# A decoder layer in split fp32: the indexer's second token half first, and 256-column fp32 products as two of 128

## The chip, the cores and the metric

The kernel runs on one core of a Trainium2 chip. The metric is the device time of one execution, in microseconds (us); lower is better.

## The reference

One layer of a hybrid decoder over 256 tokens of 2048 channels, all in float32. Cut to what matters here:

```python
h = rmsnorm(x, g_mix)
u_pool, q, k, v, q_idx, k_idx, w_idx = split(h @ w_in)
pool_out = pool_mixer(u_pool, w_pool, pool_scale)      # trailing means of 2/4/8/16 tokens, a map per group
# attention with an indexer: 16 heads of 64 score every causal key, the best 64 keys of a query stay
dots  = einsum('bqhd,bsd->bhqs', q_idx, k_idx)
score = einsum('bqh,bhqs->bqs', w_idx * idx_scale, relu(dots))
_, sel = top_k(where(causal, score, -inf), 64)
logits = einsum('bqhd,bqkhd->bhqk', q, k[sel]) * 128 ** -0.5 + bias      # 8 heads of 128
out    = einsum('bhqk,bqkhd->bqhd', softmax(logits), v[sel])
x = x + concat(pool_out, out) @ w_out
x = x + conv_ffn(rmsnorm(x, g_ffn))                    # 2048 -> 2 x 5632 -> 2048
x = x + (p @ w_ple_proj) * sigmoid(rmsnorm(x, g_ple) @ w_ple_gate)
return rmsnorm(x, g_final)
```

## The kernel before, in words

Activations lie channel-major: 128 channels on the partitions, the 256 tokens on the free axis. Exactness comes from splitting: every fp32 operand is a rounded part `hi` and a rest `lo`, both of type fp32r, and a weight tile of 128 x 128 costs two products. L147 multiplies the `hi` weights with 512 columns (hi and lo of the 256 tokens), L148 the `lo` weights with 256 columns. This pair L147, L148 makes up most of the program; a **step** below is the time from one L147 to the next with one L148 between.

Weights arrive in **units** of up to 1024 columns (512 KB, eight pairs): SyncE (SP) loads one into `raw` (four buffers), ScalarE (ACT) casts it to `hi` (L87), VectorE (DVE) subtracts to get `lo` (L88), and TensorE (PE) consumes both, from one of three `w` buffers in turn. So L147 waits for the cast of its unit and L148 for the subtraction.

The stages are, in order: v and the indexer's keys; the indexer (`query`, `score`), the q and k tiles (`qk_tile`) with the top-k on VectorE, `logits`, `softmax`; then the pool columns with the second half of `softmax`, the transposes and the products with v (`attend`), and `pool_map` (L483, twelve products of 256 columns); w_out; ffn up and down; the gate.

Three functions multiply in other shapes. `score` makes, for each of two heads, products of 128 columns (first half of the tokens) and of 256 columns (second half), in fp32r. `logits` and `attend` use operands of plain fp32; such a product stands in the profile as two instructions. The second half's `logits` (L393) have 256 columns, those of the first half 128; `attend` has one of 256 (L444) and one of 128 (L446) for each head.

The program is written as a list of operations and a scheduler decides, from its own estimate of times, in which order each engine gets them; the engines then run their lists strictly in order and wait for each other by semaphores. So an edit in one product can move others on every engine. Buffers in PSUM: four `pa` for the projections, four `ps` for everything else.

Of the kernel before, what the change touches and what calls it, by code (L numbers as in the profile page):

```python
# [18 lines left out]
P = 128  # L19
S = 256  # L20
# [30 lines left out]
def layer(ctx: ExitStack, tc: tile.TileContext, a: dict):  # L51
    nc = tc.nc
    in_order = tc.keep_in_program_order
    V, A, T, G = nc.vector, nc.scalar, nc.tensor, nc.gpsimd
# [152 lines left out]
    with ExitStack() as c1:  # L207
# [8 lines left out]
        qk = ar.tile([P, 2 * NH, S], F32, name="qk", tag="qkA")  # L216
# [43 lines left out]
        v = ar.tile([P, 2, NH * P], F32, name="v")  # L260
# [5 lines left out]
        for n in range(3):  # L266
            w = NVK if n < 2 else NVK - 80
            for t in range(2):
                vs = v[:, t, n * NVK:n * NVK + w]
# [35 lines left out]
        def score(j, qr):  # L305
            pds = [aux.tile([P, 512], F32, name="ps") for _ in range(2)]
            for e in range(2):
                for t, (o, n) in enumerate(((0, P), (P, S))):
                    q = qr[:, e, t * P:(t + 1) * P]
                    T.matmul(pds[e][:, o:o + n], q, kr[:, :n], start=True, stop=False)  # L310
                    T.matmul(pds[e][:, o:o + n], q, kr[:, S:S + n], start=False, stop=True)  # L311
            for e in range(2):
                h = 2 * j + e
                rl = ar.tile([P, 384], F32, name="rl", bufs=2)
                A.activation(rl, pds[e][:, :384], AF.Relu, scale=1.0 / 32.0)
                for t in range(2):
                    src = s0[t] if h == 0 else sc[t]
                    V.scalar_tensor_tensor(sc[t], rl[:, :P] if t == 0 else rl[:, P:],
                                           wx[:, t, h:h + 1], src, op0=OP.mult, op1=OP.add)
# [5 lines left out]
        for j in range(IH // 2):  # L325
            ps = cm_tile(a["w_qi"], j) if j else ps_q
            if j == 0:
                index_keys()
            qxs.append(query(ps))
            if j >= 2:  # L330
                score(j - 2, qxs[j - 2])
        for j in range(2):
            qk_tile(j)
            score(j + 6, qxs[j + 6])
# [53 lines left out]
        def logits(t, h0):  # L388
            n = P * (t + 1)
            hb = 512 // n  # L390
            pl = aux.tile([P, 512], F32, name="ps")
            for h in range(h0, h0 + hb):
                T.matmul(pl[:, (h - h0) * n:(h - h0 + 1) * n],  # L393
                         qk[:, 2 * h, t * P:(t + 1) * P], qk[:, 2 * h + 1, :n],
                         start=True, stop=True)
            hs = slice(h0, h0 + hb)
            V.scalar_tensor_tensor(L[t][:, hs, :], pl.rearrange("p (h s) -> p h s", s=n), P ** -0.5,
                                   tb[:, hs, S - n:], op0=OP.mult, op1=OP.add)
# [22 lines left out]
        for j in range(12, 16):  # L421
            qk_tile(j)
            if j >= 14:
                h0 = 4 * (j - 14)
# [15 lines left out]
        def attend(h, pt):  # L440
            po = aux.tile([P, 512], F32, name="ps")
            for e in range(2):
                vs = slice((h + e) * P, (h + e + 1) * P)
                T.matmul(po[:, e * S:(e + 1) * S], v[:, 0, vs], pt[:, e, :S],  # L444
                         start=e == 0, stop=False, skip_group_check=True)
                T.matmul(po[:, e * S + P:(e + 1) * S], v[:, 1, vs], pt[:, e, S:],  # L446
                         start=False, stop=e == 1, skip_group_check=True)
            po2 = po.rearrange("p (e s) -> p e s", s=S)
            split(catA[:, h:h + 2, :S], catA[:, h:h + 2, S:], po2)
# [41 lines left out]
        for i, g in enumerate((3, 2, 1, 0)):  # L491
            u = ar.tile([P, 2, PAD + S], F32, name="pu", bufs=2)
            G.memset(u[:, :, :PAD], 0.0)
            for j in range(2):
                cm_evict(u[:, j, PAD:], cm_tile(a["w_u"], 2 * g + j))
                if i < 2:
                    h0 = 4 * i + 2 * j
                    logits(1, h0)
                    softmax(1, slice(h0, h0 + 2))
                else:  # L500
                    h0 = 4 * (i - 2) + 2 * j
# [264 lines left out]
```

## Time and profile before

| | |
|---|---|
| time, median of 3 runs | 1181.37 us (1181.3 to 1181.61) |
| the profiled execution | 1181.5 us, of which the traced span is 1179.7 us |
| PE busy | 1168.7 us, 99% of the span |
| DVE, ACT busy | 855.8 us (73%), 643.8 us (55%) |
| granted TensorE clock | 0.997 in the mean: 2.4 GHz but for the first microseconds and the very end |
| DMA | 194 GB/s in the mean |

TensorE's busy time is a union of instructions that overlap in the record, so that "busy" does not say how fast it goes: what counts is the distance from the start of one product to the start of the next.

### The profile page before, as it was taken

What the parts mean: (1) busy time and instruction counts of PE and PEld (TensorE: products, weight loads), DVE (VectorE), ACT (ScalarE), POOL (GpSimd) and SP (SyncE); (2) the same over time, 40 slices, a digit from 0 to 9 for tenths busy, and PEclk for the clock granted to TensorE, in tenths of its full rate; (3) what the DMA queues carried; (4) which work ended last, traced back from release to release, by engine and by line L of the source; (5) the groups of instructions that cost most, each with busy time, mean ns of one, the idle gap of its engine ahead of it and who ended that gap; (6) DMA issues with size and microseconds to landing.
All of it is one profiled execution on the core that took longest, in us unless ns stands there. A gap on an engine that the chain in (4) does not pass through costs nothing.

```text
span 1179.7 us, 17843 instructions
## 1 busy us (share of the span) xinstructions
PE 1168.7 (99%) x6792; PEld 1035.6 (88%) x6792; DVE 855.8 (73%) x1314; ACT 643.8 (55%) x941; POOL 8.9 (1%) x27
## 2 busy tenths in 40 slices
PE   9999999999999999999999999999999999999996
PEld 9988888898888888888888888888888888888886
DVE  6578977977778888888888888888555555555564
ACT  7466444555546666666665666666444444444563
POOL 0000000000000000000000000000000000000000
PEclk9999999999999999999999999999999999999998
DMA  9656665446565555555555555556666666667662
GB/s 317 211 174 194 242 205 175 163 145 201 193 200 193 190 194 193 195 194 194 194 191 196 193 194 194 192 195 192 195 190 190 194 196 192 193 192 228 190 210 80
DMA packets 67077, 229.09 MB, mean 194 GB/s; under 512 B 7888, under 2 KB 10072, under 8 KB 66864
## 3 DMA queue, kind: packets, MB, share of 16 engines
q1 hardware_dynamic: 63840, 222.04, 58.4%
q10 hardware_dynamic: 2144, 3.28, 0.9%
q0 software_dynamic: 1008, 2.64, 0.6%
q8 instruction: 53, 0.87, 0.3%
q14 instruction: 32, 0.26, 0.1%
HBM read 224.77 MB, written 3.68 MB: 194 GB/s over the span
## 4 chain that ended last, share of the span: by engine, by line
PE 99%; DMA 0%; DVE 0%; ACT 0%; SPq 0%; POOLq 0%; issue 0%; DVEq 0%
PE pa L147 55%; PE pa L148 28%; PE pa L175 3%; PE pa L174 3%; PE pa L176 3%; PE ps L175 1%; PE ps L176 1%; PE ps L174 1%; PE ps L483 0%; PE ps L393 0%; DMA raw<-in_w_first 0%; PE ps L147 0%; PE ps L310 0%; PE ps L311 0%; PE ps L608 0%; PE ps L444 0%
## 5 line engine op out<-in xcount | busy, mean ns | idle before, releaser
L88 DVE TENSOR_TENSOR w<-raw,w 128x1024 fp32r<-128x1024 f32 (+3 forms) x420 | 503.1, 1198 | 216.3 <-ACT w L87 209.8
L147 PE MATMUL pa<-hT,w 128*128 128x512 f32 x1904 | 652.2, 390 | 0.0
L87 ACT CAST w<-raw 128x1024 fp32r<-128x1024 f32 (+3 forms) x420 | 433.3, 1032 | 339.3 <-PE pa L148 249.9
L148 PE MATMUL pa<-hT,w 128*128 128x256 f32 x1904 | 528.7, 278 | 0.0
L147 PEld LDWEIGHTS pa<-hT,w 128*128 128x128 f32 x1904 | 357.3, 188 | 74.7 <-issue 0.6
L148 PEld LDWEIGHTS pa<-hT,w 128*128 128x128 f32 x1904 | 357.9, 188 | 0.3
L147 PE MATMUL pa<-aT,w 128*128 128x512 f32 x704 | 239.4, 389 | 0.0
L148 PE MATMUL pa<-aT,w 128*128 128x256 f32 x704 | 194.3, 276 | 0.0
L147 PEld LDWEIGHTS pa<-aT,w 128*128 128x128 f32 x704 | 132.1, 188 | 27.7
L148 PEld LDWEIGHTS pa<-aT,w 128*128 128x128 f32 x704 | 132.1, 188 | 0.0
L163 ACT COPY eb<-pa 128x256 f32<-128x256 f32 x119 | 44.4, 373 | 140.2 <-PE pa L148 140.1
L164 DVE TENSOR_TENSOR eb<-pa,eb 128x256 f32<-128x256 f32 x119 | 50.3, 423 | 60.8 <-ACT eb L163 60.7
L175 PE MATMUL pa<-w,hT 128*128 128x512 f32 (+2 forms) x178 | 65.0, 365 | 0.0
L176 PE MATMUL pa<-w,hT 128*128 128x512 f32 (+2 forms) x178 | 64.6, 363 | 0.0
L174 PE MATMUL pa<-w,hT 128*128 128x512 f32 (+2 forms) x178 | 58.4, 368 | 0.1
L550 ACT ACTIVATE cv<-ub,cnv 128x256 f32<-128x256 f32 x88 | 52.8, 602 | 0.2
L147 PE MATMUL pa<-catP,w 128*128 128x512 f32 x128 | 45.9, 391 | 0.0
L147 PE MATMUL pa<-catA,w 128*128 128x512 f32 x128 | 45.6, 390 | 0.0
L554 DVE SCALAR_TENSOR_TENSOR cv<-ub,cnv,cv 128x256 f32<-128x256 f32 x88 | 42.6, 485 | 3.0
L552 DVE SCALAR_TENSOR_TENSOR cv<-ub,cnv,cv 128x256 f32<-128x256 f32 x88 | 41.9, 478 | 0.0
L165 DVE TENSOR_TENSOR ub<-eb,rbc 128x256 f32<-128x256 f32 x88 | 37.3, 425 | 2.9
L175 PEld LDWEIGHTS pa<-w,hT 128*128 128x128 f32 x178 | 33.8, 190 | 4.5 <-DVE w L88 0.6
(175 smaller groups left out, 844.7 us busy)
## 6 DMA issues: line engine op xcount, KB each, us to landing
raw<-in_w_up SPq DMA_DIRECT2D x176, 512.0 KB, 4.7
raw<-in_w_down SPq DMA_DIRECT2D x80, 512.0 KB, 4.0
raw<-in_w_qk SPq DMA_DIRECT2D x32, 512.0 KB, 4.1
raw<-in_w_out SPq DMA_DIRECT2D x32, 512.0 KB, 4.2
raw<-in_w_pg SPq DMA_DIRECT2D x32, 512.0 KB, 4.4
raw<-in_w_first SPq DMA_DIRECT2D x15, 552.0 KB, 5.1
raw<-in_w_qi SPq DMA_DIRECT2D x16, 512.0 KB, 3.8
raw<-in_w_u SPq DMA_DIRECT2D x16, 512.0 KB, 3.8
```

Of the source, the lines that this page charges most:

```text
L87: A.copy(hi, raw[:, :n])
L88: V.tensor_sub(lo, raw[:, :n], hi.bitcast(F32))
L147: T.matmul(ps, hi[:, w], act, start=first and i == 0, stop=False)
L148: T.matmul(ps[:, :S], lo[:, w], act[:, :S], start=False, stop=last and i == len(acts) - 1)
L163: A.copy(b, ps[:, S:])
L164: V.tensor_add(b, ps[:, :S], b)
L174: T.matmul(pss[t][:, :n], xh, hi[:, w], start=first and i == 0, stop=False)
L175: T.matmul(pss[t][:, :n], xh, lo[:, w], start=False, stop=False)
L176: T.matmul(pss[t][:, :n], xl, hi[:, w], start=False, stop=last and i == len(kts) - 1)
L550: A.activation(t, u[:, 2:], AF.Identity, bias=cnv[:, k + 3:k + 4], scale=cnv[:, k + 2:k + 3])
L552: V.scalar_tensor_tensor(t, u[:, 1:S + 1], cnv[:, k + 1:k + 2], t, op0=OP.mult, op1=OP.add)
L554: V.scalar_tensor_tensor(t, u[:, :S], cnv[:, k:k + 1], t, op0=OP.mult, op1=OP.add)
```

## The change

In `score` the four products of a head are issued with the second half of the tokens (256 columns) first and the first half (128 columns) last. In `logits` each product of 256 columns becomes two of 128, and in `attend` the product of 256 columns with the first half of v becomes two of 128. Sums, operands and outputs are the same.

```diff
         def score(j, qr):
             pds = [aux.tile([P, 512], F32, name="ps") for _ in range(2)]
             for e in range(2):
-                for t, (o, n) in enumerate(((0, P), (P, S))):
+                for t, o, n in ((1, P, S), (0, 0, P)):
                     q = qr[:, e, t * P:(t + 1) * P]
                     T.matmul(pds[e][:, o:o + n], q, kr[:, :n], start=True, stop=False)
                     T.matmul(pds[e][:, o:o + n], q, kr[:, S:S + n], start=False, stop=True)
...
             for h in range(h0, h0 + hb):
-                T.matmul(pl[:, (h - h0) * n:(h - h0 + 1) * n],
-                         qk[:, 2 * h, t * P:(t + 1) * P], qk[:, 2 * h + 1, :n],
-                         start=True, stop=True)
+                for k0 in range(0, n, P):
+                    c0 = (h - h0) * n + k0
+                    T.matmul(pl[:, c0:c0 + P], qk[:, 2 * h, t * P:(t + 1) * P],
+                             qk[:, 2 * h + 1, k0:k0 + P], start=True, stop=True)
...
                 vs = slice((h + e) * P, (h + e + 1) * P)
-                T.matmul(po[:, e * S:(e + 1) * S], v[:, 0, vs], pt[:, e, :S],
-                         start=e == 0, stop=False, skip_group_check=True)
+                for t in range(2):
+                    ts = slice(t * P, (t + 1) * P)
+                    T.matmul(po[:, e * S + t * P:e * S + (t + 1) * P], v[:, 0, vs], pt[:, e, ts],
+                             start=e + t == 0, stop=False, skip_group_check=True)
                 T.matmul(po[:, e * S + P:(e + 1) * S], v[:, 1, vs], pt[:, e, S:],
                          start=False, stop=e == 1, skip_group_check=True)
```

The lines behind the edits are counted on by up to three in the changed kernel (L393 is then L395, L444 is L447, L446 is L449, L483 is L486).

The scheduler gives other orders to the engines in the attention and pool stages. Two places matter below. On TensorE, around the first `pool_map` (`plr` are its inputs, `pt` and `v` those of `attend`, `L_1327` and `L_1328` the softmax of the two token halves), the list of before reads:

```order
L148 MATMUL pa<-hT,w 128x256
L483 MATMUL ps<-plr,w 128x256 x11
L434 MATMUL ps<-ident,L_1327 128x128
L435 MATMUL ps<-ident,L_1328 128x128
L436 MATMUL ps<-ident,L_1328 128x128
L444 MATMUL ps<-pt,v 128x256
L446 MATMUL ps<-pt,v 128x128
L444 MATMUL ps<-pt,v 128x256
L446 MATMUL ps<-pt,v 128x128
L483 MATMUL ps<-plr,w 128x256 x12
L147 MATMUL pa<-hT,w 128x512
```

The same place on TensorE in the changed kernel:

```order
L148 MATMUL pa<-hT,w 128x256
L435 MATMUL ps<-ident,L_1327 128x128
L436 MATMUL ps<-ident,L_1328 128x128
L437 MATMUL ps<-ident,L_1328 128x128
L447 MATMUL ps<-pt,v 128x128 x2
L449 MATMUL ps<-pt,v 128x128
L486 MATMUL ps<-plr,w 128x256 x11
L447 MATMUL ps<-pt,v 128x128 x2
L449 MATMUL ps<-pt,v 128x128
L147 MATMUL pa<-hT,w 128x512
L148 MATMUL pa<-hT,w 128x256
```

Half of the `attend` products moved ahead of the eleven `pool_map` products, and the next `pool_map` of twelve moved behind two whole units: between the eleven and the next L147 there were three transposes, four `attend` products and twelve `pool_map` products, and there are now three products of 128 columns.

On ScalarE at the same place (`catP` takes the result of a `pool_map`, `catA` that of an `attend`), before:

```order
L87 CAST w<-raw 128x512
L112 CAST plr<-pl 128x2x256
L115 ACTIVATE catP<-ps,prm 128x256
L87 CAST w<-raw 128x1024
L437 COPY pt<-ps 128x384
L112 CAST catA<-ps 128x2x256
L115 ACTIVATE catP<-ps,prm 128x256 x2
```

And in the changed kernel:

```order
L87 CAST w<-raw 128x512
L438 COPY pt<-ps 128x384
L115 ACTIVATE catP<-ps,prm 128x256
L87 CAST w<-raw 128x1024
L112 CAST catA<-ps 128x2x256
L115 ACTIVATE catP<-ps,prm 128x256
```

The cast of 1024 columns stands right behind a `catP` in both lists; it is the cast for which the L147 at the end of TensorE's rows above waits, in both kernels.

## Rows read from the trace of the kernel before

**Rows 1.** The page: span, TensorE's busy time, and the chain that ended last.

```profile
span 1179.7 us, 17843 instructions
PE 1168.7 (99%) x6792; PEld 1035.6 (88%) x6792; DVE 855.8 (73%) x1314; ACT 643.8 (55%) x941; POOL 8.9 (1%) x27
PE 99%; DMA 0%; DVE 0%; ACT 0%; SPq 0%; POOLq 0%; issue 0%; DVEq 0%
```

**Rows 2.** Stretches, L147 alone: length, PE busy (xL147), loads, clock, DMA, GB/s.

```profile
74.56:78.76 4.20, 4.19 (x12) 2.25 (x13) 1.00 0.69 219
129.16:136.64 7.48, 7.48 (x23) 4.13 (x23) 1.00 0.72 270
172.19:179.89 7.70, 7.70 (x23) 4.13 (x23) 1.00 0.53 172
213.99:227.29 13.30, 13.30 (x39) 7.14 (x39) 1.00 0.53 178
265.71:270.61 4.90, 4.89 (x14) 2.63 (x15) 1.00 0.67 219
280.07:355.55 75.48, 75.47 (x222) 41.66 (x223) 1.00 0.61 200
363.90:1076.00 712.10, 702.91 (x2068) 387.92 (x2067) 1.00 0.61 195
```

**Rows 3.** Timeline of PE in one `score`: start us, us, engine, line, operation.

```profile
79.12 0.22 PE L310 MATMUL ps<-kr,qr 128*128 128x128 f32 x1
...
79.59 0.22 PE L310 MATMUL ps<-kr,qr 128*128 128x128 f32 x1
...
80.05 0.39 PE L147 MATMUL pa<-hT,w 128*128 128x512 f32 x1
```

**Rows 4.** Timeline of PE at the logits of the second half.

```profile
212.68 1.02 PE L393 MATMUL ps<-qk 128*128 128x256 f32 x4
```

**Rows 5.** Timeline of PE at the first logits of 128 columns.

```profile
128.49 0.38 PE L393 MATMUL ps<-qk 128*128 128x128 f32 x2
```

**Rows 6.** Timeline of PE behind the first `pool_map`, up to the next unit.

```profile
232.82 0.60 PE L444 MATMUL ps<-pt,v 128*128 128x256 f32 x2
233.26 0.38 PE L446 MATMUL ps<-pt,v 128*128 128x128 f32 x2
233.48 0.60 PE L444 MATMUL ps<-pt,v 128*128 128x256 f32 x2
...
234.05 1.66 PE L483 MATMUL ps<-plr,w 128*128 128x256 f32 x12
235.55 0.39 PE L147 MATMUL pa<-hT,w 128*128 128x512 f32 x1
...
236.02 0.37 PE L148 MATMUL pa<-hT,w 128*128 128x256 f32 x1
```

**Rows 7.** Timeline of ACT at the same place.

```profile
232.71 0.48 ACT L115 ACTIVATE catP<-ps,prm 128x256 fp32r<-128x256 f32 x1
233.08 1.04 ACT L87 CAST w<-raw 128x1024 fp32r<-128x1024 f32 x1
...
235.75 0.47 ACT L115 ACTIVATE catP<-ps,prm 128x256 fp32r<-128x256 f32 x1 [0.38 <-PE ps L483]
```

**Rows 8.** Timeline of DVE at the same place.

```profile
234.27 1.21 DVE L88 TENSOR_TENSOR w<-raw,w 128x1024 fp32r<-128x1024 f32 x1
```

**Rows 9.** Timeline of PE where two L148 follow each other.

```profile
249.41 0.39 PE L147 MATMUL pa<-hT,w 128*128 128x512 f32 x1
...
249.75 0.39 PE L147 MATMUL pa<-hT,w 128*128 128x512 f32 x1
249.98 0.40 PE L148 MATMUL pa<-hT,w 128*128 128x256 f32 x2
250.21 0.40 PE L147 MATMUL pa<-hT,w 128*128 128x512 f32 x1
...
250.56 0.39 PE L147 MATMUL pa<-hT,w 128*128 128x512 f32 x1
```

## Prediction

> **What bounds the kernel.** I read the page first: TensorE is busy for 1168.7 of 1179.7 us and the chain that ended last is TensorE for 99% [rows 1]. No other engine's time is worth anything here unless it makes TensorE wait, so two questions are left: how far apart TensorE's products start, and whether the new order of the lists leaves it waiting somewhere.
>
> For the first I divided stretches of the timeline by the steps in them (one L147, one L148). The counts take in the L147 that still runs as a stretch begins, so a count of 39 is 38 steps. There are two paces. Behind the logits of the second half 22 steps take 7.70 us and 38 take 13.30: 0.350 each. From 280.07 on, 222 steps take 75.48 us: 0.340 [rows 2]. The granted clock is 1.00 (2.4 GHz) in all of these stretches, and the operations are the same. I call the steps slow and quick. A pace lasts until something other than a pair comes between. Going through the timeline from 55 to 280 us like this I count 308 slow and 206 quick steps; the first and the last of my slow stretches there are the 12 steps from 74.56 and the 14 from 265.71 [rows 2] (a few lie ahead of these), and after 280 nearly all is quick. Ten nanoseconds on 308 steps are 3.1 us, 0.26% of the span. That is all that a change of pace can give.
>
> What comes before a pace? After the first logits of 128 columns (two records at 128.49 [rows 5]) the next 22 steps take 7.48 us, quick [rows 2], and so it went four more times; these groups stand between an L147 and its L148. After groups that end in 256 columns (four records at 212.68 [rows 4]) comes the slow stretch from 213.99 [rows 2]. After an indexer group, which ends in 256 columns and stands ahead of an L147, five of seven stretches are slow. Where a group of 128-column products stands ahead of an L147, four cases of four that I found are slow. The pace is a habit I can read off, not one that I can derive.
>
> **The change part by part.**
>
> *Splitting the fp32 products.* In `attend` a product of 256 columns runs from 232.82 to 233.26, 0.44 us, and one of 128 from there to 233.48, 0.22 [rows 6]. Eight products in `logits` and eight in `attend` become 2 x 0.22 for 0.44: nothing, at most the reading error of 0.01 each. I take +0.1 us (0 to 0.2).
>
> *The indexer's order.* Four products of one head take 0.47 us (79.12 to 79.59) and those of the other 0.46 [rows 3]; the same four in another order are the same sum: 0. What they leave behind is the pace. They now end in 128 columns ahead of an L147, which I saw to be slow; five of seven stretches are slow already. Bounds: two quick stretches of 14 steps lost (+0.3 us), five slow ones of 12 to 15 made quick (-0.7). I take 0.
>
> *The logits.* Up to 213 us the groups that had 256 columns still stand between an L147 and its L148 and now hold only 128s, the form that was quick behind it. Of the slow stretches there (22, 22, 7, 12 and 17 steps, the first of them in [rows 2]) 80 steps would gain 10 ns: -0.8 us. The 38 behind 213.99 I leave slow, as one group now stands ahead of an L147. Bounds: 0 to -1.2.
>
> *The order at the first pool_map.* This is the term I trust most. In the order of before TensorE had much to do between the end of the eleven L483 and the next L147: three transposes, `attend` from 232.82 and twelve L483, up to 235.55 [rows 6]. ScalarE did the `catP` at 232.71 and the cast at 233.08, done at 234.12 [rows 7]; VectorE's subtraction went from 234.27 to 235.48 [rows 8]; L147 and L148 came at 235.55 and 236.02 [rows 6]: late by nothing, with 0.5 us to spare. In the changed lists only three products of 128 columns are left between, while the cast still stands behind a `catP`, which needs the eleven products. Call the end of the last of the eleven E. A `catP` that TensorE held up started 0.04 after the end (235.71 to 235.75 [rows 6, 7]); the cast comes 0.37 later (232.71 to 233.08) and takes 1.04 [rows 7], so it is done at E + 1.45. TensorE, whose next product starts some 0.16 ahead of a recorded end, needs 3 x 0.22 = 0.66 and would start L147 at E + 0.50: it waits 0.95. L148, which would have started at E + 0.73, needs the subtraction: E + 1.45 + 1.21 [rows 8] = E + 2.66. Together 1.9 us if VectorE is free at once. It isn't quite: two of the four `softmax` calls of the second half move from ahead of this stretch into it, and a `pu`, a `pn` and a `catP` stand ahead of the subtraction. I take 2.4 (1.9 to 2.9). Nothing gives this back: TensorE has the same work before and after it.
>
> The Trainium skill ("TensorE: Matmul & The Clock Gate", Architectural detail) states that ScalarE and VectorE are strict first-in first-out queues, while TensorE can pull weight loads forward. The trace agrees: the `catP` at 235.75 sat idle for 0.38 us on TensorE [rows 7], with nothing let past it. By this rule the stall stands and the sum is as below; if the cast could pass the `catP`, the sum would be 2.4 lower.
>
> *The w_out stage.* In both lists units are interleaved for a while there and the exit is two L148 in a row. Just ahead of 280.07 that exit turned slow into quick, for the 222 steps and more that follow [rows 2]. At 249.98 the same exit turned quick (0.34, 249.41 to 249.75) into slow (0.35, 250.21 to 250.56) [rows 9]. So if the new order comes to this exit at the quick pace, some 226 steps up to 357 us run slow: +2.3 us. I take 0, as before, but nearly as an even bet.
>
> **The sum.** 0.1 + 0 - 0.8 + 2.4 + 0 = +1.7 us on the profiled execution's 1181.5, of which the span is 1179.7. The median of the runs is 0.13 lower, 1181.37, so 1183.1.
>
> **The rivals.**
>
> *Stall and a slow w_out stage* (slower): the sum plus 2.3, +4.0, 1185.4, 0.34% up. For it: the exit that flips both ways, and a `pool_map` that now stands between an L147 and its L148 just ahead. Against it: it left quick last time. It decides once more than some 70 of those steps are slow.
>
> *The slow pace reaches the ffn.* From 363.90 to 1076 us lie over 2000 steps [rows 2]; 10 ns on each is +20 us, with the w_out stage +24: 1205. For it: no slow stretch ended by itself in the trace. Against it: small products of other shapes at 357 and 363 come between and were followed by quick steps.
>
> *No stall.* If the cast has its result early after all, by an order of events that the lists do not show, -0.7 remains, with the logits' bounds +0.2 to -1.9: about 1180.6. Faster by over 0.2% would need this and the indexer's and the 38 steps too. Against it: the wait is in the lists.
>
> *The change does nothing.* If the pace doesn't depend on the width at the end, the -0.8 is lost and the stall stays: +2.5, 1183.9.
>
> **How the numbers follow.** 0.2% is 2.36 us, about what a measurement of this kernel can tell from no change. The sum as it stands, with its bounds from +0.5 to +2.9, has 0.50 (with "the change does nothing" in its upper part), and some 0.07 of that lies over 2.36; the slow w_out stage 0.33, nearly all over; the ffn 0.05; no stall 0.12, of which 0.04 is over 2.36 us faster. So faster 0.04, same 0.53, slower 0.43. The likeliest is 1183.1, by itself 1181.9 to 1184.3. For 8 in 10 I reach to both neighbours: 1180.7 to 1186.2.
>
> **What would show it.** In the new profile: an L147 (hT) near 236 us that waits about 1 us for the cast behind a `catP`, and an L148 that waits over 1 us for the subtraction; steps of 0.340 from 172 to 213; 0.22 us for each split fp32 product; and the pace behind the last two L148 in a row. I am wrong if TensorE shows no gap there, or if the pace from 280 to 357 or behind 364 isn't 0.340.

## The result and the profile after

The changed kernel takes 1188.93 us in the median of 4 runs (1188.72 to 1189.24), the kernel before 1181.48 (1181.3 to 1181.61) beside it: a ratio of 1.0061 [1.0049, 1.0074], slower by 7.45 us. The forecast of 1183.1 was wrong, and the time lies above its range. The profiled execution took 1188.85 us with a span of 1187.0, which is 7.26 more than before. The page of the changed kernel, to be read beside [rows 1]:

```profile
span 1187.0 us, 17904 instructions
...
PE 1173.2 (99%) x6824; PEld 1038.7 (88%) x6824; DVE 855.7 (72%) x1314; ACT 643.4 (54%) x941; POOL 8.9 (1%) x27
...
PE 97%; DVE 1%; DMA 0%; issue 0%; SPq 0%; ACT 0%; POOLq 0%; DVEq 0%
```

TensorE's share of the chain fell from 99 to 97%, and VectorE now has 1% of it. That is a wait, and a wait is only 2 of the 7 us: TensorE's own busy time also grew, by 4.5 us for the same work. The page shows no more than that. The rest is in the pace, L147 alone, with the columns of [rows 2]:

```profile
81.05:85.64 4.59, 4.59 (x14) 2.43 (x14) 1.00 0.44 123
75.68:79.30 3.62, 3.62 (x12) 1.98 (x11) 1.00 0.73 233
130.29:138.01 7.72, 7.72 (x24) 4.15 (x23) 1.00 0.78 283
161.75:172.27 10.52, 10.52 (x32) 5.65 (x31) 1.00 0.56 183
185.50:190.26 4.76, 4.76 (x16) 2.63 (x15) 1.00 0.60 195
279.34:363.30 83.96, 83.96 (x240) 45.04 (x241) 1.00 0.59 193
371.25:1083.00 711.75, 702.82 (x2068) 387.89 (x2067) 1.00 0.62 195
```

The steps are counted by their start times in the timeline, as one or two L147 still run when a stretch begins. Behind the first logits 22 steps now take 7.70 us, 0.350 each, where [rows 2] had 0.340. From 279.34 on, 239 steps run at 0.350, where before 222 and more ran at 0.340. From 185.50 steps are quick, as forecast. The ffn is unchanged (711.75 us against 712.10 for the same 2068). The first row shows a third pace: 13 steps in 4.59 us, 0.353 each, in which steps of 0.350 and 0.357 take turns. The clock is 1.00 throughout.

At the first `pool_map` the timeline of TensorE shows the forecast wait (columns as in [rows 6]; the bracket is the idle time ahead and what ended it):

```profile
234.70 1.59 PE L486 MATMUL ps<-plr,w 128*128 128x256 f32 x11
236.12 0.61 PE L447 MATMUL ps<-pt,v 128*128 128x128 f32 x4
236.57 0.39 PE L449 MATMUL ps<-pt,v 128*128 128x128 f32 x2
237.78 0.49 PE L147 MATMUL pa<-hT,w 128*128 128x512 f32 x1 [0.83 <-ACT w L87]
239.05 0.39 PE L148 MATMUL pa<-hT,w 128*128 128x256 f32 x1 [0.78 <-DVE w L88]
```

ScalarE at the same place, beside [rows 7], and then VectorE, beside [rows 8]:

```profile
236.32 0.48 ACT L115 ACTIVATE catP<-ps,prm 128x256 fp32r<-128x256 f32 x1 [1.07 <-PE ps L486]
236.70 1.04 ACT L87 CAST w<-raw 128x1024 fp32r<-128x1024 f32 x1
```

```profile
236.79 0.68 DVE L463 TENSOR_TENSOR pn<-pn 128x512 f32<-128x512 f32 x1
237.39 0.48 DVE L116 SCALAR_TENSOR_TENSOR catP<-ps,prm,catP 128x256 fp32r<-128x256 f32 x1
237.79 1.21 DVE L88 TENSOR_TENSOR w<-raw,w 128x1024 fp32r<-128x1024 f32 x1
```

With the end of the eleven at 236.28 (the `catP` starts 0.04 behind it), L147 comes at E + 1.50 and L148 at E + 2.77, 2.03 us later than they would have.

Where the 7.26 us lie, by the start times of the same instructions in both traces:

| stretch | before | after | difference | forecast |
|---|---|---|---|---|
| start to the first L147 | 54.61 | 55.37 | +0.76 | 0 |
| to the k bias (L338), the indexer's part | 64.34 | 64.75 | +0.41 | 0 |
| L338 to the softmax transposes (`logits`) | 108.71 | 110.00 | +1.29 | -0.8 |
| transposes to the last `pool_map`: the stall | | | +2.03 | +2.4 |
| transposes to the last `pool_map`: the rest | | | +0.38 | +0.1 |
| last `pool_map` to the ffn's norm (`w_out`) | 91.33 | 93.55 | +2.22 | 0 |
| behind it | | | +0.16 | 0 |

### The profile page after: what moved, and what is told of

Read it like the earlier page. It is cut to its first block, busy times and chain, and to the rows that moved or that the text cites. A ratio compares the mean times of both kernels' runs of the same rounds, so it can differ in the third digit from the quotient of the medians.

```text
span 1187.0 us, 17904 instructions
## 1 busy us (share of the span) xinstructions
PE 1173.2 (99%) x6824; PEld 1038.7 (88%) x6824; DVE 855.7 (72%) x1314; ACT 643.4 (54%) x941; POOL 8.9 (1%) x27
## 4 chain that ended last, share of the span: by engine, by line
PE 97%; DVE 1%; DMA 0%; issue 0%; SPq 0%; ACT 0%; POOLq 0%; DVEq 0%
PE pa L147 55%; PE pa L148 28%; PE pa L175 3%; PE pa L176 3%; PE pa L174 3%; PE ps L176 1%; PE ps L175 1%; PE ps L174 1%; DMA raw<-in_w_first 0%; PE ps L395 0%; DVE w L88 0%; PE ps L486 0%; PE ps L147 0%; PE ps L311 0%; PE ps L611 0%; PE ps L310 0%
## 5 line engine op out<-in xcount | busy, mean ns | idle before, releaser
L147 PE MATMUL pa<-hT,w 128*128 128x512 f32 x1904 | 655.3, 391 | 0.8 <-ACT w L87 0.8
L148 PE MATMUL pa<-hT,w 128*128 128x256 f32 x1904 | 529.4, 278 | 0.8 <-DVE w L88 0.8
L147 PEld LDWEIGHTS pa<-hT,w 128*128 128x128 f32 x1904 | 357.5, 188 | 76.4 <-ACT w L87 1.0
L148 PEld LDWEIGHTS pa<-hT,w 128*128 128x128 f32 x1904 | 358.1, 188 | 1.2 <-DVE w L88 1.1
L147 PE MATMUL pa<-aT,w 128*128 128x512 f32 x704 | 239.4, 389 | 0.0
L148 PE MATMUL pa<-aT,w 128*128 128x256 f32 x704 | 194.3, 276 | 0.0
L147 PEld LDWEIGHTS pa<-aT,w 128*128 128x128 f32 x704 | 132.2, 188 | 27.6
L148 PEld LDWEIGHTS pa<-aT,w 128*128 128x128 f32 x704 | 132.2, 188 | 0.0
L174 PE MATMUL pa<-w,hT 128*128 128x512 f32 (+2 forms) x178 | 58.3, 367 | 1.1 <-ACT w L87 1.1
L147 PE MATMUL pa<-catP,w 128*128 128x512 f32 x128 | 46.8, 395 | 0.0
L147 PE MATMUL pa<-catA,w 128*128 128x512 f32 x128 | 46.5, 394 | 0.0
L174 PEld LDWEIGHTS pa<-w,hT 128*128 128x128 f32 x178 | 33.0, 190 | 5.7 <-ACT w L87 1.7
```

The costliest lines, as they stand in the source:

```text
L147: T.matmul(ps, hi[:, w], act, start=first and i == 0, stop=False)
L148: T.matmul(ps[:, :S], lo[:, w], act[:, :S], start=False, stop=last and i == len(acts) - 1)
L174: T.matmul(pss[t][:, :n], xh, hi[:, w], start=first and i == 0, stop=False)
```

## The experiments

Two theories stood against each other on the pace. **Handed on**: the pace is a state of the running chain of products, every product that is no pair turns the state that it finds into another, and a group's width does not decide by itself. **Width**, the prediction's: what a group ends in sets the pace. On the wait there were three: the cast is late because a `catP` stands ahead of it (the prediction), because VectorE's queue is (a rival), or, formed after the first two had been tried, because its buffer is.

This table has all kernels by the same stretches (us, start times of the trace): first L147 to L338, L338 to last `pool_map`, last `pool_map` to the ffn's norm. Ratios are to the kernel before in runs beside it; no ratio means a single run.

| kernel | indexer | logits to `pool_map` | w_out | time (runs) | ratio |
|---|---|---|---|---|---|
| before | 64.34 | 146.66 | 91.33 | 1181.37 (3) | |
| after | 64.75 | 150.36 | 93.55 | 1188.93 (4) | 1.0061 [1.0049, 1.0074] |
| e1_score | 64.72 | 147.74 | 91.33 | 1183.26 (10) | 1.0012 [1.0003, 1.0022] |
| e2_logits | 64.34 | 149.66 | 93.55 | 1188.56 (4) | 1.006 [1.0043, 1.0077] |
| e3_attend | 64.32 | 146.91 | 93.55 | 1183.98 (10) | 1.002 [1.001, 1.0029] |
| e4_logits_attend | 64.33 | 150.91 | 93.55 | 1187.84 (4) | 1.005 [1.0035, 1.0065] |
| f1_pair_in_w_out | 64.72 | 150.36 | 91.89 | 1187.45 (5) | 1.0048 [1.0033, 1.0063] |
| f2_one_in_w_out | 64.72 | 152.05 | 91.66 | 1187.06 (4) | 1.0042 [1.0027, 1.0058] |
| f4_other_operands | 64.60 | 150.57 | 93.77 | 1187.8 (1) | |
| g1_ident_moving | 64.75 | 150.56 | 93.77 | 1188.1 (1) | |
| g2_ident_weights | 64.60 | 152.13 | 91.66 | 1187.72 (1) | |
| g3_ident_fp32r | 64.75 | 150.56 | 91.53 | 1185.94 (1) | |
| f3_one_in_logits_stage | 64.75 | 149.40 | 93.55 | 1187.67 (4) | 1.0052 [1.0037, 1.0067] |
| s1_cast_first | 64.75 | 150.15 | 93.55 | 1187.58 (4) | 1.0046 [1.003, 1.0062] |
| s2_cast_and_sub_first | 64.60 | 150.15 | 91.33 | 1185.48 (7) | 1.0028 [1.0016, 1.0039] |
| o1_pool_weights_own | 64.72 | 147.90 | 93.91 | 1185.72 (5) | 1.0039 [1.0025, 1.0053] |
| o2_logits_pool_weights_own | 64.34 | 146.44 | 93.92 | 1183.9 (10) | 1.0021 [1.0011, 1.003] |
| o3_before_pool_weights_own | 64.33 | 146.79 | 93.72 | 1184.44 (10) | 1.0024 [1.0015, 1.0033] |
| v1_logits_own_probe | 64.35 | 146.44 | 91.58 | 1181.96 (10) | 1.0001 [0.9991, 1.001] |
| w1_before_identity | 64.78 | 147.25 | 93.58 | 1184.71 (9) | 1.0026 [1.0016, 1.0035] |

### One edit at a time: e1, e2, e3, e4

e1 has the new order in `score` alone, e2 the split in `logits`, e3 the split in `attend`, e4 both splits. Each is the kernel before with that part of the diff shown above, as in e1:

```diff
-                for t, (o, n) in enumerate(((0, P), (P, S))):
+                for t, o, n in ((1, P, S), (0, 0, P)):
```

> Only the score order is changed; logits and attend as before, and the lists of all engines are those of before but for that order. Theory (the pace of the steps is a state that small groups inside a pair hand on; the new score order leaves a slower one behind): first score to L338 takes 0.4 us more, the steps between 130 and 172 us are at 0.350 instead of 0.340 (+1.1 to +1.3), no wait at the first pool_map, w_out quick as before if the pace at 265 us is the one of before: +1.5 to +2.0 us, about 1183.1. Rival (the width in which a group ends sets the pace, as the prediction had it): the score stage moves by at most 0.4 and the steps behind the logits of 128 columns stay at 0.340: 0 to +0.4 us, about 1181.6.

> Only the logits are split; score and attend as before. The lists put the first pool_map as in the changed kernel, so L147 waits for the cast and L148 for the subtraction: +2.0 us in both theories. The lists leave the two L148 in a row of w_out where the changed kernel has them. Theory (the pace is handed on): score as before, steps from 129 to 172 us at 0.340 as before, then as the groups of changed form hand it on; if w_out is entered as in the changed kernel its 240 steps are slow (+2.2): +3 to +4.5 us in all, about 1185. Rival (the width at the end): steps quick from 129 to 213 us (-0.8), the stall +2.0, w_out open: +1.2, or +3.4 if w_out is slow.

> Only attend is split; score and logits as before. By the lists no wait at the first pool_map; the exit of the interleaved units in w_out is that of the changed kernel. Both theories: nothing changes up to 228 us and no stall: 0 +- 0.2. Then the pace at which TensorE comes to the two L148 in a row decides: it comes quick and leaves slow, +2.2 us (1183.6), or comes slow and leaves quick, 0 (1181.4).

> Both splits with the old score order: on every engine the lists of the changed kernel but for the order inside score. The stall (2.0 us) and the w_out exit are then those of the changed kernel. Theory (the pace is handed on): the score order's own +0.4 and the slow steps that it leaves from 130 to 172 us (+1.2) are gone, so 1.5 to 2.4 us under the changed kernel, about 1186.9. Rival (the width at the end): the score order costs only its +0.4, so 1188.5. If the +0.8 of the start stage belongs to the changed kernel's program and not to its run, it is here too; else another 0.8 less.

**e1** is the clean one. TensorE's list equals that of before but for the order inside `score`, ScalarE's is the same, on VectorE three pairs of neighbours change places, and TensorE waits for nothing in either trace between 60 and 400 us. Its `logits` are the ones of before. Yet behind the first logits it goes as the changed kernel does (L147 alone):

```profile
129.88:137.60 7.72, 7.72 (x24) 4.15 (x23) 1.00 0.77 279
```

These are 22 steps of 0.350, where [rows 2] had 7.48 us at the quick pace for the same instructions. The difference to before grows by 0.39 us up to L338 and by 1.08 from there to the transposes, all of it between the first logits and 172 us. Ahead of the first logits the steps of before alternate between 0.350 and 0.357, those of e1 and of the changed kernel between 0.352 and 0.348. In before, L147 alone ahead of them (23 steps of 0.353):

```profile
120.14:128.25 8.11, 8.11 (x24) 4.30 (x24) 1.00 0.44 154
```

So the order in `score` left another state, L338 made the slow pace of it and not the third, and the same lone logits product kept the slow pace, where in before it had turned the third into quick. This is one trace of e1, but every kernel bears it out: the pace ahead of the first logits (in f3 ahead of its added product) is slow in the 12 with the new order and third in 7 of the 8 with the old one; the eighth, w1, adds a product there. Over before, after and e1 to e4 I classed what stood ahead of and behind each lone logits product of 128 columns inside a pair: quick stayed quick 20 times, slow stayed slow 18 times, the third pace became quick 7 times, and nothing else occurred. (In all twenty traces it is 52, 92 and 22, again without an exception.) The width theory falls here.

**e2** comes to the first logits as before does and is quick behind them (21 steps from 130.53 to 137.67, 0.340 each). It reaches the transposes only 0.06 us later than before, so the split in `logits` costs nothing by itself. It has the wait, which is longer here, as only one product of 128 columns instead of three stands between the eleven and the next L147:

```profile
236.85 0.50 PE L147 MATMUL pa<-hT,w 128*128 128x512 f32 x1 [1.27 <-ACT w L87]
238.11 0.39 PE L148 MATMUL pa<-hT,w 128*128 128x256 f32 x1 [0.76 <-DVE w L88]
```

It has the slow w_out too. The split of `logits` alone brings about the scheduler's new order that makes the wait; a slow w_out comes with the order that either split brings about, as e3 shows.

**e3** has no wait, is as before up to the transposes, and is then slow in w_out, with L147 alone:

```profile
274.10:358.00 83.90, 83.90 (x240) 44.99 (x241) 1.00 0.60 194
```

**e4** has both splits and the order of before in `score`; with the +0.41 and the +1.08 missing it should have been 1.5 us ahead of the changed kernel. From the first L147 to the end it takes 1131.74 us, the changed kernel 1131.61. Three stretches around its wait, L147 alone (the granted clock is the number third from the end):

```profile
234.00:236.60 2.60, 0.50 (x2) 0.31 (x2) 1.00 0.54 178
236.60:240.20 3.60, 3.54 (x6) 1.80 (x7) 0.53 0.49 173
240.20:243.30 3.10, 3.10 (x10) 1.62 (x9) 1.00 0.00 1
```

Behind the same two waits of 0.83 and 0.78 us the clock fell to about its lower level of 1.2 GHz, four steps took 0.64 us instead of 0.35 and the one on either side 0.53 and 0.56, 1.6 us more in all, which hid the 1.5. Of the timed runs the one at a mean clock of 0.997 took 1186.75 us, near the forecast, and the three at 0.996 took 1187.77 to 1188.24. In the profile of the changed kernel the clock stays at 1.00 there. The Trainium skill ("TensorE: Matmul & The Clock Gate", What's actually happening) has the clock at one of two levels by how busy TensorE was of late, and says that the moment varies from run to run. The traces agree that it varies, 0.53 in one and 1.00 in the other behind waits of equal length; here it is whether the clock falls at all.

### What turns the pace in w_out: f1, f2, f4, g1, g2, g3

Each adds a small product or two, whose result nothing reads, inside one pair of the slow w_out stretch of the changed kernel (the fifth pair of the unit `c` = 4, `h` = 0). f1 adds two products with the form of L139 (a broadcast times the identity), f2 a single one of fp32; f4, g1 and g2 have that product with other operands in the same place, g3 the identity in fp32r (the labels behind the lines are added here; f1's lines are left out):

```diff
-            T.matmul(ps, hi[:, w], act, start=first and i == 0, stop=False)
+            T.matmul(ps, hi[:, w], act, start=first and i == 0, stop=False); then(i)
...
+                in_order(T.matmul(px[:, :P], ident, ident, start=True, stop=True))            # f2
+                in_order(T.matmul(px[:, :P], v[:, 0, :P], v[:, 1, :P], start=True, stop=True))  # f4
+                in_order(T.matmul(px[:, :P], v[:, 0, :P], ident, start=True, stop=True))        # g1
+                in_order(T.matmul(px[:, :P], ident, v[:, 1, :P], start=True, stop=True))        # g2
+                in_order(T.matmul(px[:, :P], idr, idr, start=True, stop=True))                  # g3
```

The first operand is the weights, the second what moves through them.

> The changed kernel with one group more: two products of 128 columns (identity with a broadcast column, the form of L139, four records) into a spare buffer, between an L147 and its L148 at the fifth product pair of the ninth unit of w_out, near 284.5 us; their result is read by nothing. Theory (the pace is a state that groups hand on; this form left quick behind it from slow in the changed kernel at 370 us): the 226 or so steps up to 364 us go from 0.350 to 0.340, -2.3 us, the group costs +0.4: 1187.0. Rival (the slow w_out belongs to its place, its operands or transfers, not to what came before): all stays at 0.350, +0.4: 1189.3.

> The same place in the changed kernel, but one plain fp32 product of 128 columns (identity with identity, two records, the form of a single logits product); its result is read by nothing. Theory (this form keeps the pace that it finds): 0.350 before and after it, +0.22 us: 1189.1. Rival (the prediction's rule: a group inside a pair that ends in 128 columns leaves the quick pace): 226 steps at 0.340, -2.3 + 0.2: 1186.9.

> The run f2 with another operand pair: at the same place in w_out the one product is of two different 128 x 128 blocks of v instead of identity with identity. Theory A (a lone fp32 product flips the slow pace of w_out, whatever its data): 211 steps at 0.340 behind it, as in f2. Theory B (that both operands are one buffer, or the identity, makes the difference to the logits products, which kept the slow pace): 0.350 until 364 us, 2.1 us more between the last pool_map and L202 than in f2.

> The run f2 with the identity only as the moving operand and a block of v as the weights (read by nothing). Identity with identity left 0.340 behind it (f2), v with v left 0.350 (f4). If the moving operand decides: 0.340 from 288 to 364 us. If the weights decide, or both must be the identity: 0.350, 2.1 us more between the last pool_map and L202 than in f2.

> The run f2 with the identity only as the weights and a block of v as the moving operand. If the weights decide: 0.340 from 288 to 364 us. If the moving operand decides, or both must be the identity: 0.350.

> The run f2 with the identity as fp32r (one more cast early in the program), so that the product is a single record of some 0.06 us instead of two of 0.11. If the identity as such decides: 0.340 from 288 to 364 us at a cost of 0.06 to 0.1, which would pay behind every group that leaves 10 slow steps or more. If the plain fp32 product's two records matter: 0.350 or the third pace.

f1 turned slow into quick: from 289.47 to 361.20 us 211 steps run at 0.340. So did f2 with one product, against my theory that a lone product keeps the pace. L147 alone behind that product, in f2:

```profile
291.27:363.00 71.73, 71.73 (x213) 39.59 (x212) 1.00 0.60 196
```

In g1 (weights from `v`, the identity moving), which is as slow as f4 (both operands from `v`; steps of 0.350 as well):

```profile
288.83:363.30 74.47, 74.47 (x214) 39.89 (x213) 1.00 0.58 191
```

In g2 (the identity as weights, `v` moving):

```profile
291.07:363.00 71.93, 71.93 (x213) 39.66 (x212) 1.00 0.62 195
```

With the same place, shape and type, the identity as weights turns the pace and a block of `v` doesn't, and whether `v` or the identity moves does not matter. f4, g1, g2 and g3 are one run each, but f2's product turned slow into quick in f3 and v1 as well, and the lone logits products, whose weights are a block of `q`, left slow as it was 92 times of 92. The identity isn't the only operand that does it: in f1 the weights are a broadcast column, and there it was two products. In fp32r (g3) it does the same in one instruction instead of two, and the w_out stage is then 2.0 us shorter than in the changed kernel. Whether it is the identity's many zeros or where it lies in memory isn't told apart by these runs. What they do show is that w_out's +2.2 us is the pace and nothing else: f1 is as the changed kernel up to the last `pool_map` and 1.66 us shorter behind it.

### The same product ahead of the logits: f3

f3 puts f2's product into the changed kernel between the first L338 and the first logits:

```diff
+            cm_evict(qk[:, j, :], cm_tile(a["w_qk"], j, probe if j == 2 else lambda i: None))
```

> The changed kernel with one identity product of 128 columns more (the product of the run f2, read by nothing), inside a pair 12 steps behind L338, near 124.4 us, where the changed kernel runs at 0.350 until 172 us through four single logits products that all kept that pace. Theory A (the identity product breaks the slow pace wherever it stands, and a single logits product keeps what it finds): the 140 steps from there to 172 us are quick, -1.4 + 0.24, the start of the group of four products at 172 comes 1.2 us earlier behind the first indexer product than in the changed kernel. Theory B (what made w_out quick in f2 was its place or its operands, not the product): they stay at 0.350, +0.24.

L147 alone ahead of the product, behind the first logits, and behind the fourth:

```profile
120.50:124.30 3.80, 3.80 (x12) 2.02 (x11) 1.00 0.57 193
129.54:137.00 7.46, 7.46 (x23) 4.11 (x23) 1.00 0.78 276
160.17:170.40 10.23, 10.23 (x32) 5.66 (x31) 1.00 0.55 181
```

Ten steps of 0.350 ahead of it, 0.340 behind it (20 steps, and 29 of them in the third row), and four logits products in turn kept that. The time from the first logits to 172 us is shorter by about 1.15 us than in the changed kernel, what the order in `score` had cost there (1.14 in e1); in all, the stage from L338 to the last `pool_map` is 1.0 us shorter, as later groups hand on another state. The stretch is the one in e1, turned the other way by an edit ahead of it: handed on again.

### The wait: s1, s2, o1

s1 moves both `catP` of the first `pool_map` behind the cast in the changed kernel; s2 also moves a `pn` and the `catP` on VectorE behind the subtraction.

```diff
+                    ah = A.activation(catP[:, kt, :S], pd, AF.Copy, scale=col)
+                    if pin:
+                        in_order(ah)
...
+                then = (lambda h: late(True) if h == 0 else None) if (i, j) == (2, 1) else lambda h: None
```

> The changed kernel with the first evacuation to catP traced and pinned behind the next unit's cast, so that on ScalarE the cast of 1024 columns stands ahead of catP and on VectorE the subtraction stands ahead of catP too; the work is the same. The prediction's account (the cast behind catP is what holds both L147 and L148): the wait of 2.0 us goes, 1186.9. Rival (VectorE's own queue holds L148 as well: in the changed kernel a pu and a pn run there until 237.4, only 0.4 before the subtraction started): L147 doesn't wait, L148 waits some 1.5 us, -0.4 in all, 1188.5. Pace behind it open by +-0.5.

> As the run before, and the last pn of that pooling is traced behind the subtraction, so that the subtraction stands right behind a pu. By the rival of the run before (VectorE's queue) the subtraction starts near 236.8 and the wait that is left is about 1.0 us, by the prediction's account none. The lists change behind this place: w_out is left over the two L148 in a row of the kernel before (226 steps behind them). Theory on the pace: whichever pace it brings there, the steps from 284 to 360 us are all of one pace: 1.0 us less than the changed kernel if slow (1187.9), 3.2 less if quick (1185.7).

Both accounts missed. In s1 the `catP` no longer stands ahead of the cast on ScalarE, and still the cast waits, as ScalarE's timeline shows:

```profile
233.76 0.48 ACT L438 COPY pt<-ps 128x384 f32<-128x384 f32 x1
235.31 1.05 ACT L87 CAST w<-raw 128x1024 fp32r<-128x1024 f32 x1 [1.07 <-PE ps L486]
```

It is the cast itself that now waits for the last of the eleven `pool_map` products, for 1.07 us. The cast reads none of their results; it writes a `w` buffer, and there are three of these, one of which holds the weights that the eleven still read. TensorE's timeline in s1:

```profile
236.41 0.50 PE L147 MATMUL pa<-hT,w 128*128 128x512 f32 x1 [0.47 <-ACT w L87]
237.67 0.38 PE L148 MATMUL pa<-hT,w 128*128 128x256 f32 x1 [0.76 <-DVE w L88]
```

With E at 235.27 these are E + 1.14 and E + 2.40: of the 2.03 us that TensorE lost, the place of the `catP` accounts for 0.37, the time from the start of the `catP` to that of the cast behind it. s2 has the same 0.47 and 0.76; its VectorE is idle ahead of the subtraction, so that VectorE's queue isn't the cause either:

```profile
237.16 1.22 DVE L88 TENSOR_TENSOR w<-raw,w 128x1024 fp32r<-128x1024 f32 x1 [0.53 <-ACT w L87]
```

From the first L147 to the end s2 takes 1128.86 us, 2.75 less than the changed kernel, and 2.22 of that is another matter: its w_out is 91.33, as in before.

o1 tests the buffer: the changed kernel, with the weights of `pool_map` in buffers of their own (in memory that `score` used earlier), so that the three `w` buffers serve the rest.

```diff
-            hi, lo = unit(a["w_pool"][g], 512)
+            hi, lo = unit(a["w_pool"][g], 512, own=ar)
```

> The changed kernel with the pool_map weights (hi and lo of w_pool) in a buffer of their own instead of one of the three w buffers; the work is the same, the lists change from the pool stage on. Theory (the cast of the next unit waits for the w buffer that the late pool_map products still read, so no order on ScalarE or VectorE could free it): no wait of L147 or L148 near 236 us, 2.0 us less than the changed kernel and no fall of the granted clock in any run: 1186.9 if w_out is slow, 1184.6 if it is quick. Rival (the queues on ScalarE and VectorE hold it): at least 1.2 us of waits stay there, 1188.1 or 1185.8.

TensorE has no wait at all between 200 and 300 us. All engines in two stretches, of which the first number behind the length is TensorE's busy time:

```profile
230.00:245.00 15.00, 15.00 (x102) 13.70 (x101) 14.47 (x28) 11.11 (x21) 0.43 (x4) 1.00 0.56 179
245.00:262.00 17.00, 17.00 (x125) 15.88 (x124) 14.89 (x26) 10.08 (x19) 0.00 (x0) 1.00 0.51 164
```

The stage up to the last `pool_map` is 2.46 us shorter than in the changed kernel. The scheduler's lists change with this edit too, so that the run alone does not prove the buffer to be the cause. That the cast waits for the buffer rests on the 1.07 us of s1 and on the code: the `w` buffers are taken in turn, and the unit of that cast is the third behind that of the `pool_map`. The buffer freed with the order left as it was is not tested; by the prediction's sum the `catP` alone would then hold the cast for as long. The Trainium skill ("Perfetto Trace Analysis", Optimization Strategy) takes a gap that repeats on the engine that should be saturated as a hint that the next tile finds no free buffer. Here it was a single gap, and the runs agree with that reading of it: 2.03 us lost with three buffers for both uses, none with buffers apart, where the order had changed as well.

### Versions without the wait: o2, o3, v1, w1

o2 is the split in `logits` alone with o1's buffers, o3 the kernel before with them, as a control. v1 is o2 with f2's product in w_out (`c` = 2). w1 is the kernel before with a cheaper product in six places, the identity in fp32r times a column of zeros, added to the sum (the first line below is v1's, the second w1's):

```diff
+                      probe if (c, h) == (2, 0) else lambda i: None)
...
+            T.matmul(ps[:, :P], idr, zr[:, 0:1].to_broadcast([P, P]), start=False, stop=False)
```

> Only the logits split (old score order, attend as before), with the pool_map weights in a buffer of their own. Theory (the split itself is worth nothing but the pace that it leaves, the stall was the scheduler's order meeting the buffer): no wait near 236 us, the score and logits stages as in the run with the logits alone, 1181.5 to 1182.4 if w_out is quick, 2.3 more if it is slow. Rival (the split products cost time by themselves): slower than the kernel before by over 1 us up to the first transposes.

> The kernel before with the pool_map weights in a buffer of their own: a control for the buffer, since the kernel before had no wait at the first pool_map. Theory: up to the pool stage as before; behind it only the pace differs, 1181.5 +- 0.8 if w_out is quick, 2.3 more if it is slow. Rival (the third w buffer was short of one unit in other places too): at least 0.5 us less than before with the same paces.

> The best that the runs point to: the logits split alone, the pool_map weights in a buffer of their own, and one identity product inside a pair at the entry of w_out (read by nothing), 4 steps behind its two L147 in a row. That kernel without the product had its last pool_map 0.2 us earlier than the kernel before (from the same start) and then 262 slow steps. If the product flips them: -2.5 + 0.24, level with the kernel before to -0.2 us (1181.3 to 1181.8 beside 1181.5). If it doesn't: 1184.1.

> The kernel before with six more products, fp32r identity as weights and a column of zeros (broadcast to 128) as the moving operand, added to the running sum inside a pair: 1 step behind L338, behind the 256-column logits at 189, 201 and 213 us, behind the last eleven pool_map products and behind the two L148 in a row of w_out. All lists are otherwise those of before. Theory (the weights decide, g2, and the fp32r form flips at some 0.12 us each, g3): the stretches of 23, 22+7, 12+17, 38 and 11 steps or more behind them run at 0.340, -1.2 us, the six products cost 0.7, the last two of them perhaps for nothing: 0.5 to 0.9 us less than before, 1180.6 to 1181.0 beside 1181.4. Rival (the moving data or its zeros matter as well): the paces stay and the products cost 0.7: 1182.1.

o2 is level with before up to the last `pool_map` (146.44 against 146.66), so that with the wait gone the split in `logits` isn't slower; its w_out is slow by 2.6 us. So is o3's, by 2.4, in which nothing of the change is left: its lists bring it to two L148 in a row (at 269.65 us) in another state. v1 turns that stretch (256 steps from 270.75 to 357.80 at 0.340) and is level with before, 1.0001 [0.9991, 1.001]. That is the best that I found; no version beat the kernel before.

w1 was to make the kernel before quicker and made it slower by 2.85 us. Of its six products three left the quick pace and three the slow one. One of each, L147 alone:

```profile
215.08:228.00 12.92, 12.92 (x39) 7.13 (x39) 1.00 0.56 183
...
284.28:359.50 75.22, 75.22 (x216) 40.36 (x216) 1.00 0.59 192
```

So the identity as weights doesn't always leave the quick pace: with zeros moving it left either, and at 283.68 us, in w_out, it left slow as it was, which g3's did not. The indexer of w1 takes 64.78 us instead of 64.34 although TensorE's list is that of before up to L338, so that the list alone doesn't fix the pace. All twenty traces show the same further ahead: behind the L139 near 61 us, reached at 0.340 in all, by the same products and without a wait, the next steps are slow in 10, third in 7 and quick in 3. The two small tiles that w1 adds move others of the same pool in memory; that addresses are part of the state is a guess from this, not shown.

## Why the prediction was wrong

The sum of +1.7 fell short by 5.55 us of the table: 2.22 in w_out, 2.09 in the logits' stretch, 0.76 ahead of the first L147, 0.41 in the indexer and 0.44 in the rest, less 0.37 by which the stall was smaller. What failed is the pace.

**The logits** were forecast at -0.8 us and measured +1.29. The step that failed is "the groups now hold only 128s, the form that was quick behind it". In before, the first of these products stood behind the third pace, which I had taken for the slow one, and a lone product of 128 columns turns that into quick; it leaves slow as it is (18 of 18). I had read off what follows a group without what precedes it. A counterexample stood in the trace of before: a lone product of 128 columns that was reached at the slow pace, and the 7 slow steps behind it were even among the 80 that I wanted to gain:

```profile
197.22 0.39 PE L147 MATMUL pa<-hT,w 128*128 128x512 f32 x1
...
197.57 0.40 PE L147 MATMUL pa<-hT,w 128*128 128x512 f32 x1
197.80 0.38 PE L393 MATMUL ps<-qk 128*128 128x128 f32 x2
...
198.14 0.40 PE L147 MATMUL pa<-hT,w 128*128 128x512 f32 x1
...
198.49 0.39 PE L147 MATMUL pa<-hT,w 128*128 128x512 f32 x1
```

With the split alone (e2) the stretch took +0.06 us and not -0.8: some of its groups left quick and others, quick before, left slow. f3 shows the same products quick when they are reached at the quick pace.

**The indexer's order** was forecast at 0 and cost +0.41 by itself and, by what it handed on, most of the logits' +1.29 (e1: 0.39 and 1.08). My bounds of -0.7 to +0.3 ended at the indexer, as if a pace stopped where its stage does.

**The w_out stage**, +2.22 for a forecast of 0, was the nearly even bet, and it fell the other way. The rival "stall and a slow w_out stage" named the place and the price (2.3) rightly. The evidence against it, "it left quick last time", was misread: the steps ahead of that exit in before alternate between 0.350 and 0.357, the third pace, not the slow one, as TensorE's timeline in before shows:

```profile
278.56 0.40 PE L147 MATMUL pa<-catA,w 128*128 128x512 f32 x1
...
278.91 0.40 PE L147 MATMUL pa<-catA,w 128*128 128x512 f32 x1
...
279.26 0.40 PE L147 MATMUL pa<-catP,w 128*128 128x512 f32 x1
...
279.61 0.40 PE L147 MATMUL pa<-catP,w 128*128 128x512 f32 x1
```

Here, as at 249.98 [rows 9], the exit of two L148 was reached at the quick pace. TensorE's timeline there in the changed kernel:

```profile
278.76 0.28 PE L148 MATMUL pa<-catP,w 128*128 128x256 f32 x1
278.87 0.39 PE L147 MATMUL pa<-catP,w 128*128 128x512 f32 x1
279.10 0.28 PE L148 MATMUL pa<-catP,w 128*128 128x256 f32 x1
279.21 0.28 PE L148 MATMUL pa<-catA,w 128*128 128x256 f32 x1
279.33 0.40 PE L147 MATMUL pa<-catA,w 128*128 128x512 f32 x1
```

The steps up to 279.10 are 0.340, those behind 0.350. Wherever two L148 follow each other behind at least two steps in the twenty traces, a last step of 0.340 ahead of them was followed by the slow pace in 18 cases of 18. Behind the third pace it depends on which of its two steps came last: quick in 8 of 8 after 0.350, slow in 3 of 3 after 0.357. Twice (o2, v1) slow turned into quick. So what this exit makes of the quick pace stood in the trace of before; that the new order would come to it at the quick pace could not be read from the lists, and the loss of the bet is in part bad luck.

**The stall** was right in its place and its size, 2.03 us for 2.4 (1.9 to 2.9), and the sum E + 1.45 and E + 2.66 for L147 and L148 came out as E + 1.50 and E + 2.77. Its reason was half of the truth. The cast did stand behind the `catP` and start when that let it, which agrees with the first-in first-out rule cited; but the term's cause, "the cast still stands behind a `catP`", was not the only hold. Taking the `catP` away frees 0.37 of the 2.03 us (s1), as the cast would have waited for the end of the eleven as well, for its buffer. The allowance of 0.5 for VectorE was too much: the subtraction started 0.05 behind the end of the cast.

**Splitting the products** cost next to nothing, as forecast: in the rows of the changed kernel two products of `attend` take 0.45 us (236.12 to 236.57), 0.22 each. **The ffn** rival did not come about.

**Not foreseen** are +0.76 us ahead of the first L147, where the changed kernel's page shows L174 waiting 1.1 us for a cast. The edits aren't there, and over all kernels, whose TensorE work there is the same, the first L147 falls anywhere from 53.95 to 55.75 us; what decides it stays open. The 0.16 us behind w_out are 15 steps at 0.350 instead of 0.340; the other 0.38 behind the transposes, where the orders differ, I did not take apart.

## What to carry to other kernels

When a kernel's main products run at more than one pace with the clock unchanged, note the pace on both sides of every interruption, as a change far upstream can come out as time lost far downstream. For a forecast wait list all that the instruction needs, the last reader of the buffer that it writes among them, since taking away the one cause that is in view may leave the wait. And waits of 1.6 us in all can cost as much again by the clock behind them, in some executions only (e4).

## What the hardware showed that I had not expected

- The same pairs L147, L148 at 2.4 GHz run in steps of 0.340, 0.350 or 0.353 us, the first two for hundreds of steps on end (239 at 0.350 in the changed kernel), until something other than a pair comes between.
- A single product of 128 columns can turn that pace, and its weights matter for whether it does: the identity turned slow into quick (f2, g2, g3), a block of `v` in the same place didn't (f4, g1). It is no tool to rely on, as w1 shows. The list of products alone doesn't fix the pace (near 61 us the same products left all three), and what the state is made of stays open.
- Two waits of 0.83 and 0.78 us, 0.4 us of work between them, were followed by the lower clock in the profiles of e4, f2 and g2 (0.53 in e4, 0.50 in f2 from 238.80 to 242.00) and by the full clock in those of the changed kernel, f1, f3, g1 and g3; so were the 1.27 and 0.76 of e2 and the 0.83 and 0.82 of f4. The timed runs of f3 agree with a cost that comes and goes, 1186.9 and 1187.0 us at a mean clock of 0.997 and 1188.3 and 1188.9 at 0.995. Those of e2 and f1 don't: e2's shortest, 1187.61, is at 0.995, and f1's longest, 1188.48, at 0.997.
